# Root mean squares by products with ones on all partitions, and low-key score products over all 128 rows, in a two-layer hybrid decoder

## The chip, the cores and the metric

The kernel runs on one core of a Trainium2 chip. The metric is the device time of one execution of the whole program in microseconds, as a median over runs.

## The reference, cut to what matters

Two decoder layers are applied to a prompt of 1024 tokens and to 8 sample sequences of 4 tokens with 1024 cached ones each. A layer computes a normed input, one combined input projection, four token mixers, four branch projections merged with gates, an output projection and a normed residual. The change touches the root mean square (in the output norm, the next layer's input norm, the per-token layer norm of the convolution branch, and each head of attention) and the scores of the differential attention for the prompt:

```python
def _rms(x, g):
    y = x * lax.rsqrt(jnp.mean(x * x, axis=-1, keepdims=True) + EPS)
    return y * g

def block(args):          # 128 queries, 4 heads, two maps j of width 64
    sc = jnp.einsum('bqhjd,bkhjd->bhjqk', qi, k) * ATTN_SCALE
    sc = jnp.where(kpos <= qpos, sc, -jnp.inf)
    p = jax.nn.softmax(sc, axis=-1)
    return einsum('bhqk,bkhe->bqhe', p[:, :, 0] - lam * p[:, :, 1], v)

o = _rms(attend(q, k, v, lam), g_subln) * (1.0 - lam_init)
```

## The kernel before

Tokens stand in three groups of 352 columns (TB; prompt and samples together make 1056), features on the 128 partitions. TensorE works in fp32 rounded to a shorter format (fp32r) for nearly all of its products, and accuracy comes from splitting: a value is a high part (rounded) and a low part (the rest), and a product is high times high, low times high and high times low. `gemm` (L238) issues such products, `three` lists them, and the tiles `whi_t`, `wlo_t`, `hh_t`, `hl_t` hold the parts of weights and tokens. The weights' ring splits each 128 x 1024 block on ScalarE (L210) and VectorE (L211).

The order of the work on each engine but SyncE is made when the program is built: a scheduler plays the program through on a timeline of its own costs and writes each engine's row of instructions. TensorE then runs its row strictly in order. The source code decides dependences and priorities, and generators (`side`, `step_side`) feed attention and decode between the projections' products. `pace` adds an order between two TensorE products without a wait on data.

Attention of one head is `attn(h)`. `a_part(qb)` makes the scores of 128 queries against n = 128 (qb + 1) keys, in tiles S[0] and S[1] of PSUM for the two maps. The queries and keys of map j lie in `qs[j]` and `ks[j]` over 128 rows: the product takes the high and low parts of the queries against the high keys in one pass. The mask is added by a product of an identity with a mask tile (`identr`, `maskr`). What is missing is the high queries against the low keys. The low keys of both maps share one tile `kl`, map 0 in rows 0 to 63 and map 1 in rows 64 to 127, so this third product has 64 rows for each map, and the two maps' products stand last, beside each other. There are 4 heads of 8 blocks in each of the 2 layers, 64 blocks in all. In six of the eight heads the two maps' low products stand together on TensorE; in the third head of each layer, which runs beside decode, they stand singly.

`rstd_of` gives 1/rms for every column. Before, TensorE multiplies 128 or 88 columns at a time with a vector of ones (L349, in fp32), which puts the sums of squares on partitions; ScalarE takes the square root (L351), VectorE the reciprocal (L352), its high and low part (L355, L356) and two diagonal matrices (L360), and two products of ones with these (L364) spread the result over all partitions. It is called 16 times in attention (512 columns), 6 times each in the layer norm (L1097) and the output norm (L1216), three times for the next layer's input norm (L1223), three times at the start (L1260) and four times in decode (L793, 64 columns). In attention the squares are taken on ScalarE behind each output product (L623).

Of the kernel before, what the change touches and what calls it, by code (L numbers as in the profile page):

```python
# [98 lines left out]
def step_kernel(ctx, tc, xT, wst, wada, kc, vc, ptab, stp, sts, stc, cT, vecs, wpool, lamqk, cst, rope,  # L99
# [221 lines left out]
    def make_A(l, k=0, n=KC):  # L321
        g = cv("g_pre", l, k, n).unsqueeze(2).to_broadcast([P, n, 9])
        ve.scalar_tensor_tensor(out=Am[:, k:k + n], in0=modT[l][:, 8 + k:8 + k + n], scalar=1.0, in1=g, op0=ALU.add, op1=ALU.mult)
# [18 lines left out]
    def rstd_of(x, n, scale, dg, pb=None):  # L342


        w = max(w_ for w_ in (P, TB // 4, 64) if n % w_ == 0)
        m = n // w
        pc = ms(m)[:w]
        for j in range(m):
            te.matmul(out=pc[:, j:j + 1], lhsT=x[:, j * w:(j + 1) * w], rhs=ones[:, 0:1], start=True, stop=True)  # L349
        r = const("rsm", 8, bufs=2)[:w, 0:m]  # L350
        sc.activation(out=r, in_=pc, func=AF.Sqrt, bias=epsc[:w], scale=scale)  # L351
        ve.reciprocal(out=r, in_=r)  # L352
        rs = [r] if len(dg) == 1 else [const(f"rsm{i}", 8)[:w, 0:m] for i in range(2)]
        if len(dg) == 2:
            ve.tensor_copy(out=R(rs[0]), in_=r)  # L355
            ve.tensor_tensor(out=R(rs[1]), in0=r, in1=rs[0], op=ALU.subtract)  # L356
        cast = R if len(dg) == 2 else lambda ap: ap
        for r, d in zip(rs, dg):
            d = d[:w].rearrange("p (j t) -> p j t", t=w)
            ve.tensor_tensor(out=cast(d), in0=ident[:w, :w].unsqueeze(1).to_broadcast([w, m, w]),  # L360
                             in1=r.unsqueeze(2).to_broadcast([w, m, w]), op=ALU.mult)
        pb = ms(n) if pb is None else pb
        for i, d in enumerate(dg):
            te.matmul(out=pb, lhsT=cast(ones[:w]), rhs=cast(d[:w]), start=i == 0, stop=i == len(dg) - 1)  # L364
        return pb
# [57 lines left out]
    def setup_lambda(l, lq):  # L423
# [9 lines left out]
        for o, name, f, w in ((0, "pool_scale", 0.5, 4), (4, "g_cnorm", 0.5, 4), (8, "b_cnorm", 0.5, 4),  # L433
                              (12, "g_subln", 0.5 * (1.0 - lam_init), 1)):
# [4 lines left out]
    def layer(l, pos, hh, hl, begun, psB):  # L439
# [120 lines left out]
        def attn(h):  # L560
            E = [[ep(f"e{2 * i + j}", 1024) for j in range(2)] for i in range(2)]
            wt = [ep(f"e{4 + i}", 4, 256) for i in range(4)]
            od, msq = ep("od", 1056), ep("ms", 1024)
# [4 lines left out]
            def a_part(qb):  # L568
# [5 lines left out]
                chunks = [(c0, min(512, n - c0)) for c0 in range(0, n, 512)]  # L574
                for j in range(2):
                    for c0, w in chunks:
                        c = slice(c0, c0 + max(w, 256))
# [6 lines left out]
                for c0, w in chunks:  # L584
                    c = slice(c0, c0 + max(w, 256))
# [30 lines left out]
            def pv(s):  # L616
# [6 lines left out]
                sc.activation(out=msq[:, s * 256:s * 256 + 256], in_=pb, func=AF.Square)  # L623
# [28 lines left out]
        def decode(p):  # L652
# [428 lines left out]
        def layernorm():  # L1081
            for b in range(3):
# [14 lines left out]
                rs = rstd_of(s2, TB, 1.0 / 512, [lnp("ls1", TB), lnp("ls3", TB)])  # L1097
# [343 lines left out]
```

## Time and profile before

| | |
|---|---|
| median of 3 runs | 3004.43 us (3002.55 to 3007.85) |
| profiled execution, its own time | 3002.23 us |
| its span in the trace | 3000.4 us |
| granted TensorE clock, mean | 0.989 of full speed |
| HBM read, written | 240.73 MB, 36.34 MB |
| instructions in the span | 46185 |

In the views that follow, PE is TensorE's products, PEld its weight loads, DVE VectorE, ACT ScalarE, POOL GpSimd and SP SyncE. A row of a timeline has the start in us, the busy time of the group, the engine, the line, the operation, output and inputs by the program's tile names, for products rows x columns of the weights, the output's shape, and the count of instructions. A group of "lines" ends with busy time in us and the mean duration of one in ns, then the idle time of the engine ahead of them and what ended it. Products on TensorE overlap in a pipeline, so busy times of neighbouring rows overlap as well, and starts are the surer measure. A product in plain fp32 is recorded as two, since it makes two passes.

### The profile page before, as it was taken

The page shows a single profiled execution, that of the slowest core. Times are in us where ns is not written, and L with a number is a line of the kernel's source. Part 1 is how long each engine was busy: PE and PEld are TensorE (multiplying, and loading weights), DVE is VectorE, ACT ScalarE, POOL GpSimd, SP SyncE. Part 2 cuts the span into 40 slices and gives each one's busy share as a digit, 9 for nine tenths or more (in the row PEclk, how much of TensorE's full clock was granted, in tenths as well). Part 3 has the DMA queues.
Part 4 walks back from the last instruction along what each step waited for, and adds up shares of the span by engine and source line. Part 5 has one row for each costly group of instructions (what it writes and reads, how often), then busy time and mean ns, then how long its engine had stood idle before and what let it go on. Part 6 is the DMA issues. An engine that isn't in the chain of part 4 may idle for free.

```text
span 3000.4 us, 46185 instructions
## 1 busy us (share of the span) xinstructions
PE 2913.8 (97%) x18436; PEld 2781.6 (93%) x18436; DVE 1634.2 (54%) x2540; ACT 970.6 (32%) x1904; POOL 495.1 (17%) x642
## 2 busy tenths in 40 slices
PE   6999999999999999999989999999999999999998
PEld 4899889989999999999989998998899999999998
DVE  7756356577972145323487663664889522543233
ACT  4544245313112123212454551542221121322132
POOL 3221011012200111011230120101140001110123
PEclk8999999999999999999999999999999999999999
DMA  6122621362233223222321236115511221221122
GB/s 230 48 65 85 203 78 53 116 196 64 67 109 105 80 86 96 97 75 71 108 98 48 67 118 205 49 45 153 179 38 59 84 76 43 80 90 57 50 69 97
DMA packets 135961, 280.08 MB, mean 93 GB/s; under 512 B 18338, under 2 KB 88994, under 8 KB 134210
## 3 DMA queue, kind: packets, MB, share of 16 engines
q10 hardware_dynamic: 45072, 145.74, 15.9%
q1 hardware_dynamic: 79778, 90.73, 9.7%
q0 software_dynamic: 10896, 40.67, 3.6%
q8 instruction: 145, 2.38, 0.3%
q14 instruction: 70, 0.57, 0.1%
HBM read 240.73 MB, written 36.34 MB: 92 GB/s over the span
## 4 chain that ended last, share of the span: by engine, by line
PE 84%; DVE 7%; DMA 2%; issue 2%; SPq 2%; ACT 2%; POOL 0%; DVEq 0%; ACTq 0%; POOLq 0%
PE mm_t L238 45%; PE m_t L238 28%; PE s_t L238 3%; PE ms_t L238 2%; DVE acc_t L954 2%; SPq L671 1%; PE ms_t L611 1%; PE s_t L776 1%; DVE wlo_t L211 1%; PE s_t L702 1%; DVE acc_t L373 1%; DMA e_t<-in_kc_dram 1%; PE ms_t L349 1%; PE b_t L238 1%; ACT rop_t L497 1%
## 5 line engine op out<-in xcount | busy, mean ns | idle before, releaser
L238 PE MATMUL mm_t<-hh_t,whi_t 128*128 128x352 f32 x2792 | 533.3, 329 | 5.8 <-ACT hh_t L385 2.1
L238 PE MATMUL mm_t<-hh_t,wlo_t 128*128 128x352 f32 x2792 | 528.6, 327 | 0.0
L238 PE MATMUL mm_t<-hl_t,whi_t 128*128 128x352 f32 x2792 | 524.0, 325 | 0.0
L211 DVE TENSOR_TENSOR wlo_t<-wst_t,whi_t 128x1024 fp32r<-128x1024 f32 x203 | 268.5, 1329 | 455.6 <-ACT whi_t L210 455.4
L238 PEld LDWEIGHTS mm_t<-hh_t,whi_t 128*128 128x128 f32 x2792 | 458.7, 190 | 27.6 <-issue 14.6
L238 PEld LDWEIGHTS mm_t<-hh_t,wlo_t 128*128 128x128 f32 x2792 | 460.5, 189 | 9.7 <-issue 8.2
L238 PEld LDWEIGHTS mm_t<-hl_t,whi_t 128*128 128x128 f32 x2792 | 458.7, 189 | 6.7 <-issue 5.6
L954 DVE SCALAR_TENSOR_TENSOR acc_t<-uc_t,vec_t,acc_t 128x1024 f32<-128x1024 f32 x240 | 320.4, 1360 | 1.6
L1164 POOL TENSOR_TENSOR mg_t<-mg_t,th_t 128x352 f32<-128x352 f32 x144 | 144.7, 1008 | 925.8 <-DVE th_t L1163 925.7
L210 ACT ACTIVATE whi_t<-wst_t 128x1024 fp32r<-128x1024 f32 x203 | 213.3, 1056 | 246.7 <-PE mm_t L238 163.6
L238 PE MATMUL m_t<-hh_t,wlo_t 128*128 128x352 f32 x1352 | 249.7, 325 | 0.0
L238 PE MATMUL m_t<-hl_t,whi_t 128*128 128x352 f32 x1352 | 247.6, 324 | 0.0
L238 PE MATMUL m_t<-hh_t,whi_t 128*128 128x352 f32 x1352 | 246.4, 323 | 0.0
L238 PEld LDWEIGHTS m_t<-hh_t,wlo_t 128*128 128x128 f32 x1352 | 223.6, 190 | 0.9
L238 PEld LDWEIGHTS m_t<-hl_t,whi_t 128*128 128x128 f32 x1352 | 222.7, 189 | 0.0
L238 PEld LDWEIGHTS m_t<-hh_t,whi_t 128*128 128x128 f32 x1352 | 222.0, 189 | 0.1
L1072 ACT ACTIVATE th_t<-m_t 128x352 f32<-128x352 f32 x114 | 52.6, 463 | 373.4 <-PE m_t L238 362.5
L1072 ACT ACTIVATE th_t<-mm_t 128x352 f32<-128x352 f32 x78 | 35.9, 463 | 272.0 <-PE mm_t L238 240.9
L590 DVE TENSOR_REDUCE sml_t<-s_t 128x1 f32<-128x256 f32 (+7 forms) x128 | 92.4, 752 | 53.1 <-PE s_t L238 52.7
L593 ACT ACTIVATE e_t<-s_t,sml_t 128x256 f32<-128x256 f32 (+7 forms) x128 | 94.3, 744 | 69.7 <-DVE sml_t L591 39.9
L238 PE MATMUL m_t<-yh_t,whi_t 128*128 128x352 f32 x460 | 94.5, 326 | 0.0
L238 PE MATMUL m_t<-yh_t,wlo_t 128*128 128x352 f32 x460 | 93.1, 324 | 0.0
(349 smaller groups left out, 3854.0 us busy)
## 6 DMA issues: line engine op xcount, KB each, us to landing
wst_t<-in_wst_dram ACTq DMA_DIRECT2D x209, 512.0 KB, 3.6
e_t<-in_kc_dram SPq DMA_DIRECT2D x224, 128.0 KB, 3.0
e_t<-in_vc_dram SPq DMA_DIRECT2D x216, 128.0 KB, 2.6
rld_t<-ysp_t ACTq DMA_DIRECT2D x16, 528.0 KB, 4.5
wa_t<-in_wada_dram SPq DMA_DIRECT2D x16, 512.0 KB, 10.4
wlo_t<-in_wada_dram ACTq DMA_DIRECT2D x16, 512.0 KB, 3.7
whi_t<-in_wada_dram ACTq DMA_DIRECT2D x16, 512.0 KB, 4.3
x_t<-in_xT_dram SPq DMA_DIRECT2D x3, 1408.0 KB, 6.0
```

Of the source, the lines that this page charges most:

```text
L210: sc.activation(out=R(hi), in_=st, func=AF.Copy)
L211: (eng or ve).tensor_tensor(out=R(lo), in0=st, in1=hi, op=ALU.subtract)
L238: last_mm[0] = m = te.matmul(out=out, lhsT=R(lh), rhs=R(rh), start=first and i == 0, stop=last and i == n - 1)
L349: te.matmul(out=pc[:, j:j + 1], lhsT=x[:, j * w:(j + 1) * w], rhs=ones[:, 0:1], start=True, stop=True)
L373: ve.tensor_reduce(out=acc[:, i], in_=o.rearrange("p k n -> p n k"), axis=AX.X, op=ALU.add)
L497: sc.activation(out=sw[32 * (g ^ 1):32 * (g ^ 1) + 32], in_=pb[32 * g:32 * g + 32], func=AF.Copy)
L590: ve.tensor_reduce(out=s[:, j:j + 1], in_=S[j][:, :n], axis=AX.X, op=ALU.max)
L593: sc.activation(out=E[qb % 2][j][:, :n], in_=S[j][:, :n], func=AF.Exp, bias=s[:, 2 + j:3 + j], scale=0.125, accum_out=s[:, 4 + j:5 + j])
L611: te.transpose(out=pb[:, k], in_=e0[:, (k0 + k) * P:(k0 + k + 1) * P], identity=ident)
L954: pace(ve.scalar_tensor_tensor(out=a, in0=v, scalar=w(k), in1=a, op0=ALU.mult, op1=ALU.add))
L1072: sc.activation(out=th[:, b * TB:(b + 1) * TB], in_=pb, func=AF.Tanh, scale=0.5)
L1164: gp.tensor_tensor(out=mg[:, d, cl], in0=mg[:, d, cl], in1=th, op=ALU.add)
```

## The change

Scores: a tile `qz` of 128 rows holds the high queries of map j in that map's rows and zeros in the other map's rows. GpSimd clears it once for each head, and ScalarE copies the queries of the block into it, two copies for each block. The low-key product of map j then runs over all 128 rows of `kl`, and stands directly behind that map's product and mask. It is no longer ordered by `pace` behind both maps. `qz` lies in the tile "ms", which held the squares.

Root mean squares: the squares x are scaled and rounded on ScalarE (high part), VectorE makes the low part, and two products with a full matrix of ones put the sum of each column on all partitions (L356). For the start and decode there is one fp32 product with ones and a scale. ScalarE takes the inverse square root and its square, and VectorE makes one Newton step in place, in PSUM; the factor -0.5 of that step is moved into the following multiplications and constants. In attention the squares are now taken over 512 columns at the end of the head, out of the attention output `od`.

```diff
-    def rstd_of(x, n, scale, dg, pb=None):
-        w = max(w_ for w_ in (P, TB // 4, 64) if n % w_ == 0)
...
-        for j in range(m):
-            te.matmul(out=pc[:, j:j + 1], lhsT=x[:, j * w:(j + 1) * w], rhs=ones[:, 0:1], start=True, stop=True)
...
-        sc.activation(out=r, in_=pc, func=AF.Sqrt, bias=epsc[:w], scale=scale)
-        ve.reciprocal(out=r, in_=r)
...
-        for i, d in enumerate(dg):
-            te.matmul(out=pb, lhsT=cast(ones[:w]), rhs=cast(d[:w]), start=i == 0, stop=i == len(dg) - 1)
+    def rstd_of(x, scale, parts, yt, pb=None):
...
+        if parts:
+            hi, lo = parts
+            sc.activation(out=R(hi), in_=x, func=AF.Copy, scale=scale)
+            ve.scalar_tensor_tensor(out=R(lo), in0=x, scalar=scale, in1=hi, op0=ALU.mult, op1=ALU.subtract)
+            for i in range(2):
+                te.matmul(out=pb, lhsT=R(ones), rhs=R(parts[i]), start=i == 0, stop=i == 1)
+        else:
+            te.matmul(out=pb, lhsT=ones, rhs=x, start=True, stop=True)
+            ve.tensor_scalar(out=pb, in0=pb, scalar1=scale, scalar2=None, op0=ALU.mult)
+        sc.activation(out=y, in_=pb, func=AF.Abs_reciprocal_sqrt, bias=epsc)
+        sc.activation(out=t, in_=y, func=AF.Square)
+        ve.scalar_tensor_tensor(out=pb, in0=pb, scalar=EPS, in1=t, op0=ALU.add, op1=ALU.mult)
+        ve.scalar_tensor_tensor(out=pb, in0=pb, scalar=-3.0, in1=y, op0=ALU.add, op1=ALU.mult)
...
+            qz = ep("ms", 1024)[:, 0:512].rearrange("p (i j q) -> p i j q", i=2, j=2)
+            gp.memset(qz, 0.0)
...
+                for j in range(2):
+                    r = slice(64 * j, 64 * j + 64)
+                    sc.activation(out=R(qz[r, qb % 2, j]), in_=qs[j][r, q1], func=AF.Copy)
                 for j in range(2):
...
                         gemm(S[j][:, c], [(qs[j][:, q1], ks[j][:, c])], last=False)
-                    gemm(S[j][:, q1], [(identr, maskr)], first=False, last=False)
+                        if c is chunks[-1]:
+                            gemm(S[j][:, q1], [(identr, maskr)], first=False, last=False)
+                        gemm(S[j][:, c], [(qz[:, qb % 2, j], kl[:, c])], first=False)
                     if j == 0:
                         yield
-                hi = last_mm[0]
-                for c0, w in chunks:
...
-                    for j in range(2):
-                        r = slice(64 * j, 64 * j + 64)
-                        gemm(S[j][:, c], [(qs[j][r, q1], kl[r, c])], first=False, on=hi)
...
-                sc.activation(out=msq[:, s * 256:s * 256 + 256], in_=pb, func=AF.Square)
...
+                msq = ep(f"e{4 + i}", 1024)[:, 0:512]
+                sc.activation(out=msq, in_=o[:, c], func=AF.Square)
+                rs = rstd_of(msq, 1.0 / P, two(dg), two(yt))
```

Since a scheduler sets the rows, three places show what moved. First TensorE in the third head of the first layer, beside decode's products (`s_t<-e_t` are decode's, `mm_t` are the projection's, `k_t`, `maskr_t` and `kl_t` the score's, `x8` counts equal products in a row). Before:

```order
L238 MATMUL mm_t<-hl_t,whi_t 128x352 x7
L238 MATMUL s_t<-k_t,q_t 128x256
L238 MATMUL s_t<-maskr_t,identr_t 128x128
L238 MATMUL s_t<-kl_t,q_t 128x256
L238 MATMUL mm_t<-hl_t,whi_t 128x352
L238 MATMUL mm_t<-hh_t,whi_t 128x352 x6
L776 MATMUL s_t<-e_t 32x256 x8
L238 MATMUL mm_t<-hh_t,whi_t 128x352 x2
L238 MATMUL mm_t<-hh_t,wlo_t 128x352 x8
```

Now, in the same head:

```order
L238 MATMUL mm_t<-hh_t,wlo_t 128x352 x3
L238 MATMUL s_t<-k_t,q_t 128x256
L238 MATMUL s_t<-maskr_t,identr_t 128x128
L238 MATMUL s_t<-kl_t,ms_t 128x256
L238 MATMUL s_t<-k_t,q_t 128x256
L238 MATMUL s_t<-maskr_t,identr_t 128x128
L238 MATMUL s_t<-kl_t,ms_t 128x256
L238 MATMUL mm_t<-hh_t,wlo_t 128x352 x5
L238 MATMUL mm_t<-hl_t,whi_t 128x352
L611 MATMUL ms_t<-cs_t,e_t 128x128
```

A map used to stand by itself between decode's products; now both maps of a block stand together, with nothing of decode's between, and the low-key product reads the tile of zeros (`ms_t`).

Second, ScalarE in the first head, where the exponentials (L593) follow the scores. Before:

```order
L210 ACTIVATE whi_t<-wst_t 128x1024
L506 ACTIVATE k_t<-rop_t 64x352 x2
L593 ACTIVATE e_t,sml_t<-s_t,sml_t 128x128 x2
L541 ACTIVATE vcm_t<-mm_t 128x352
L210 ACTIVATE whi_t<-wst_t 128x1024
L506 ACTIVATE q_t<-tbb_t 64x352 x2
```

Now, with the query copies (L580):

```order
L210 ACTIVATE whi_t<-wst_t 128x1024
L580 ACTIVATE ms_t<-q_t 64x128 x2
L541 ACTIVATE vcm_t<-mm_t 128x352
L210 ACTIVATE whi_t<-wst_t 128x1024
L593 ACTIVATE e_t,sml_t<-s_t,sml_t 128x128 x2
L506 ACTIVATE k_t<-rop_t 64x320 x2
L513 ACTIVATE knew_t<-rop_t 128x32
L497 ACTIVATE tbb_t<-mm_t 32x352 x4
L210 ACTIVATE whi_t<-wst_t 128x1024
L580 ACTIVATE ms_t<-q_t 64x128 x2
L593 ACTIVATE e_t,sml_t<-s_t,sml_t 128x256
```

The copies of a block stand behind a weights' copy (L210), and in the second block ahead of the exponentials.

Third, TensorE at the end of the first layer, the output norm of the last group of tokens (`ada_t`). Before:

```order
L349 MATMUL ms_t<-ones_t,ssq_t 88x1 x4
L238 MATMUL mm_t<-hh_t,whi_t 128x352 x8
L238 MATMUL mm_t<-hh_t,wlo_t 128x352 x8
L238 MATMUL mm_t<-hl_t,whi_t 128x352 x8
L238 MATMUL mm_t<-hh_t,whi_t 128x352 x8
L238 MATMUL mm_t<-hh_t,wlo_t 128x352 x8
L364 MATMUL ada_t<-acc_t,ones_t 128x352
L238 MATMUL mm_t<-hl_t,whi_t 128x352 x2
L364 MATMUL ada_t<-acc_t,ones_t 128x352
```

Now:

```order
L356 MATMUL ada_t<-parts_t,ones_t 128x352
L238 MATMUL mm_t<-hh_t,whi_t 128x352 x8
L238 MATMUL mm_t<-hh_t,wlo_t 128x352 x8
L238 MATMUL mm_t<-hl_t,whi_t 128x352 x8
L238 MATMUL mm_t<-hh_t,whi_t 128x352 x5
L356 MATMUL ada_t<-parts_t,ones_t 128x352
L238 MATMUL mm_t<-hh_t,whi_t 128x352 x3
```

The four column products are gone, and the two halves of the remaining product, which stood two products apart at the end, now stand 29 products apart.

More of the change, by code (lines that the diff above doesn't have):

```diff
@@ L322, in make_A @@
         g = cv("g_pre", l, k, n).unsqueeze(2).to_broadcast([P, n, 9])
-        ve.scalar_tensor_tensor(out=Am[:, k:k + n], in0=modT[l][:, 8 + k:8 + k + n], scalar=1.0, in1=g, op0=ALU.add, op1=ALU.mult)
+        a = Am[:, k:k + n]
+        ve.scalar_tensor_tensor(out=a, in0=modT[l][:, 8 + k:8 + k + n], scalar=1.0, in1=g, op0=ALU.add, op1=ALU.mult)
+        ve.tensor_scalar(out=a, in0=a, scalar1=-0.5, scalar2=None, op0=ALU.mult)
     def make_G(l):
@@ L340, in two @@
         return [t[:, 0], t[:, 1]]
[L342 to L364 removed]
+    def rstd_of(x, scale, parts, yt, pb=None):
+        n = x.shape[-1]
+        y, t = yt
+        pb = ms(n) if pb is None else pb
+        if parts:
[11 more added lines that the diff above has]
+        ve.scalar_tensor_tensor(out=pb, in0=pb, scalar=-3.0, in1=y, op0=ALU.add, op1=ALU.mult)
         return pb
@@ L644, in attn @@
                 c = slice(i * 512, i * 512 + 512)
-                dg = ep(f"e{i}", 1024)
-                rs = rstd_of(msq[:, c], 512, 1.0 / P, two(dg.rearrange("p (i n) -> p i n", i=2)))
+                dg, yt = [ep(f"e{i + x}", 1024).rearrange("p (i n) -> p i n", i=2) for x in (0, 2)]
+                msq = ep(f"e{4 + i}", 1024)[:, 0:512]
+                sc.activation(out=msq, in_=o[:, c], func=AF.Square)
+                rs = rstd_of(msq, 1.0 / P, two(dg), two(yt))
                 ve.tensor_tensor(out=o[:, c], in0=o[:, c], in1=rs, op=ALU.mult)
@@ L789, in decode @@
             sc.activation(out=fin, in_=pb, func=AF.Copy)
-            sqd, rsd = wn[:, 0:64], wn[:, 64:128]
+            sqd, yd = wn[:, 0:64], wn[:, 64:128]
             sc.activation(out=sqd, in_=pb, func=AF.Square)
             yield
-            ve.tensor_tensor(out=fin, in0=fin, in1=rstd_of(sqd, 64, 1.0 / P, [rsd]), op=ALU.mult)
+            ve.tensor_tensor(out=fin, in0=fin, in1=rstd_of(sqd, 1.0 / P, None, (yd, qf)), op=ALU.mult)
             ve.scalar_tensor_tensor(out=fin, in0=fin, scalar=hv[:, l, 12:13],
@@ L1096, in layernorm @@
                 yield from skip(6)
-                rs = rstd_of(s2, TB, 1.0 / 512, [lnp("ls1", TB), lnp("ls3", TB)])
-                ve.tensor_tensor(out=x, in0=x, in1=rs.unsqueeze(1).to_broadcast([P, 4, TB]), op=ALU.mult)
+                rs = rstd_of(s2, 1.0 / 512, [lnp(f"lr{i}", TB) for i in range(2)], [t[:, i] for i in range(2)])
+                ve.scalar_tensor_tensor(out=x, in0=rs.unsqueeze(1).to_broadcast([P, 4, TB]), scalar=-0.5, in1=x,
+                                        op0=ALU.mult, op1=ALU.mult)
                 for c in range(4):
@@ L1215, in layer @@
                 ve.tensor_tensor(out=scols(ob[:, :, n:]), in0=scols(ob[:, :, n:]), in1=samp(GG), op=ALU.mult)
-            rs = rstd_of(ssq, TB, 1.0 / D, two(op("acc", 2, TB)), psM("ada", 512)[:, 0:TB])
+            rs = rstd_of(ssq, 1.0 / D, two(op("parts", 2, TB)), two(op("yt", 2, TB)), psM("ada", 512)[:, 0:TB])
             for d in range(0, KC, 2):
                 o_, x_ = ob[:, d:d + 2], xb[:, d:d + 2]
-                ve.tensor_tensor(out=o_, in0=o_, in1=rs.unsqueeze(1).to_broadcast([P, 2, TB]), op=ALU.mult)
+                ve.scalar_tensor_tensor(out=o_, in0=rs.unsqueeze(1).to_broadcast([P, 2, TB]), scalar=-0.5, in1=o_,
+                                        op0=ALU.mult, op1=ALU.mult)
                 (gp if d % 4 else ve).tensor_tensor(out=x_, in0=x_, in1=o_, op=ALU.add)
@@ L1222, in layer @@
                 gp.dma_start(out=xmid[b], in_=xb)
-                rs = rstd_of(sumsq(xb, ob, op("acc", 2, TB)), TB, 1.0 / D, two(op("acc", 2, TB)))
+                rs = rstd_of(sumsq(xb, ob, op("acc", 2, TB)), 1.0 / D, two(op("parts", 2, TB)), two(op("yt", 2, TB)))
                 for t, x in zip(nh, "hl"):
```

12 lines of the change are left out of this document (5 added, 7 removed).

## The prediction

> **What bounds the kernel now.** I read the page first, then the busy time by stages, then TensorE's timeline at each kind of work that the change touches, then the groups by line for the prices on the other engines, and last the end of the program. The page, engines' busy time:
>
> ```profile
> PE 2913.8 (97%) x18436; PEld 2781.6 (93%) x18436; DVE 1634.2 (54%) x2540; ACT 970.6 (32%) x1904; POOL 495.1 (17%) x642
> ```
>
> and its chain of work that ended last:
>
> ```profile
> PE 84%; DVE 7%; DMA 2%; issue 2%; SPq 2%; ACT 2%; POOL 0%; DVEq 0%; ACTq 0%; POOLq 0%
> ```
>
> PE works for 97% of the span and makes 84% of the chain. So a microsecond taken off PE's row of work comes off the end, as long as the other engines keep up; and steps added to DVE or ACT cost nothing unless PE stands waiting for them. The busy time by stages (columns: busy time of PE, PEld, DVE, ACT, POOL, granted clock, DMA share, GB/s) for the end of the first layer and the stretch behind it:
>
> ```profile
> 1440.00:1500.00 60.00, 60.00 (x385) 59.98 (x384) 28.67 (x41) 25.75 (x47) 16.72 (x15) 1.00 0.27 93
> 1500.00:1600.00 100.00, 88.30 (x533) 84.33 (x533) 82.00 (x153) 55.84 (x125) 33.05 (x45) 0.93 0.27 93
> ```
>
> Inside a layer PE has no gap at all. At the transition between layers it stands idle for 11.7 us of 100 and DVE is busy for 82: there, longer chains on DVE and ACT do show.
>
> **Low-key products: what goes.** TensorE's timeline in the second head, first where the two maps of a block stand together over 256 keys, then over 640 keys (512 and 256 columns). Columns: start, busy time, operation, tiles, rows times columns of the weights, output, count. Busy times of pipelined products overlap, so I take start to start:
>
> ```profile
> 199.62 1.46 PE L238 MATMUL mm_t<-hl_t,whi_t 128*128 128x352 f32 x8
> 200.92 0.28 PE L238 MATMUL s_t<-k_t,q_t 128*128 128x256 f32 x1
> 201.03 0.23 PE L238 MATMUL s_t<-maskr_t,identr_t 128*128 128x128 f32 x1
> 201.09 0.33 PE L238 MATMUL s_t<-k_t,q_t 128*128 128x256 f32 x1
> 201.26 0.22 PE L238 MATMUL s_t<-maskr_t,identr_t 128*128 128x128 f32 x1
> 201.41 0.38 PE L238 MATMUL s_t<-kl_t,q_t 64*128 64x256 f32 x2
> 201.73 1.56 PE L238 MATMUL mm_t<-hh_t,whi_t 128*128 128x352 f32 x8
> 203.13 1.46 PE L238 MATMUL mm_t<-hh_t,wlo_t 128*128 128x352 f32 x8
> ...
> 227.74 0.51 PE L238 MATMUL s_t<-k_t,q_t 128*128 128x512 f32 x2
> 228.09 0.22 PE L238 MATMUL s_t<-maskr_t,identr_t 128*128 128x128 f32 x1
> 228.24 0.61 PE L238 MATMUL s_t<-kl_t,q_t 64*128 64x512 f32 x4
> 228.78 1.08 PE L238 MATMUL mm_t<-hh_t,wlo_t 128*128 128x352 f32 x5
> 229.70 0.60 PE L611 MATMUL ms_t<-cs_t,e_t 128*128 128x128 f32 x4
> ```
>
> A plain product of 352 columns takes 1.30/8 = 0.162 us, one of 256 columns 0.11 to 0.12, 512 and 256 together 0.35, so one of 512 takes 0.23; for 384 I take 0.18, between them. A mask product ahead of a full-row product takes 0.06 (201.03 to 201.09); ahead of 64-row products it takes 0.15 (201.26 to 201.41; 228.09 to 228.24). So entering costs 0.09. The pair of 64-row products takes 0.32 (201.41 to 201.73), where one full-row product of that width takes 0.12: 0.20 on top. Behind them eight products take 1.40 instead of 1.30, five take 0.92 instead of 0.81: leaving costs 0.10 to 0.11. Together about 0.40 us for a group. The wider pairs bear it out: 0.54 against 0.35, again 0.19 on top.
>
> In the third head of each layer the maps stand singly, with one 64-row product in a group:
>
> ```profile
> 403.94 0.22 PE L238 MATMUL s_t<-maskr_t,identr_t 128*128 128x128 f32 x1
> 404.09 0.38 PE L238 MATMUL s_t<-kl_t,q_t 64*128 64x256 f32 x1
> 404.40 0.58 PE L238 MATMUL mm_t<-hh_t,whi_t 128*128 128x352 f32 x2
> 404.82 0.97 PE L238 MATMUL mm_t<-hh_t,wlo_t 128*128 128x352 f32 x5
> ```
>
> Again 0.15 ahead, 0.31 within, and 0.42 for two products instead of 0.32. A single costs as much as a pair, so the pair runs side by side in the array, and that is what the change gives up. There are 6 heads with 8 joined blocks and 2 heads with 16 single maps, 80 groups: 80 x 0.40 = 32.0 us go. In the 6 joined heads each pair becomes two products in a row. The blocks' widths, 256 twice, 384, 512, 512+256 twice, 512+384 and 512+512, make 0.12 + 0.12 + 0.18 + 0.23 + 0.35 + 0.35 + 0.41 + 0.46 = 2.22 us a head, 13.3 in all. In the third heads nothing is added. **Net: -18.7 us.**
>
> This is also where a rule stands for and against. By the Trainium skill's page "TensorEngine Tiling (Array Packing)", section Tiling Modes, a change of tiling mode drains TensorE, while tiles of one mode work independently. The rows show both: 0.09 ahead and 0.10 behind, and a pair for the price of a single. By the second half alone (a pair is free parallelism to be kept) the sum of the low-key part would be +13.3 instead of -18.7.
>
> **Root mean squares on PE.** In attention, at the end of the fourth head (four columns in two passes each make eight records):
>
> ```profile
> 561.29 0.95 PE L349 MATMUL ms_t<-ones_t,ms_t 128*128 128x1 f32 x8
> 562.10 1.54 PE L238 MATMUL mm_t<-hl_t,whi_t 128*128 128x352 f32 x8
> ...
> 567.02 0.39 PE L364 MATMUL ms_t<-e_t,ones_t 128*128 128x512 f32 x1
> 567.26 0.50 PE L349 MATMUL ms_t<-ones_t,ms_t 128*128 128x1 f32 x4
> ```
>
> and for the tokens at the layer transition:
>
> ```profile
> 1533.30 0.71 PE L349 MATMUL ms_t<-ones_t,ssq_t 128*88 128x1 f32 x8
> 1534.02 1.56 PE L238 MATMUL mm_t<-hh_t,whi_t 128*128 128x352 f32 x8
> 1535.41 1.46 PE L238 MATMUL mm_t<-hh_t,wlo_t 128*128 128x352 f32 x8
> ...
> 1540.58 0.33 PE L364 MATMUL ada_t<-acc_t,ones_t 88*128 88x352 f32 x1
> 1540.75 0.49 PE L238 MATMUL mm_t<-hl_t,whi_t 128*128 128x352 f32 x2
> ```
>
> A call in attention spends 0.81 on the columns and 2 x 0.24 on spreading the result; the new one spends two products of 512 columns, 0.46. Saved: 0.83, times 16 calls (8 heads, two halves) 13.3 us. A token call loses its 0.72; its two spreading products (0.17 each) are replaced by two of the same width (0.162). With 6 layer norms and 6 output norms that is 12 x 0.72 = 8.6. Leaving fp32 costs the products behind it 1.39 - 1.30 = 0.09; in the two orders PE passes from fp32 back to rounded products 177 times before and 143 after: 34 x 0.09 = 3.1. The 3 norms of the next layer's input may give up to 2 more, which I leave at zero, as they stand where PE waits anyway; the start and decode calls trade like for like. **Net: -25.0 us.**
>
> **Other engines.** The nearest rows for the new steps are the same forms elsewhere, a rounding copy and the rest of it for 352 columns, and the weights' copy that may stand ahead of them:
>
> ```profile
> L1133 ACT ACTIVATE hh_t<-mg_t 128x352 fp32r<-128x352 f32 x48 | 20.6, 488 | 21.6 <-POOL mg_t L1164 14.9 <-PE mm_t L238 3.4 <-PE m_t L238 3.4
> L1134 DVE SCALAR_TENSOR_TENSOR hl_t<-mg_t,hh_t 128x352 fp32r<-128x352 f32 x48 | 24.0, 552 | 9.9 <-ACT hh_t L1133 9.9
> L210 ACT ACTIVATE whi_t<-wst_t 128x1024 fp32r<-128x1024 f32 x203 | 213.3, 1056 | 246.7 <-PE mm_t L238 163.6 <-PE m_t L238 82.1 <-DMA od_t<-in_vc_dram 0.5
> ```
>
> A call has copy, rest, two products, inverse root, square and two DVE steps in a row: 0.49 + 0.55 + 0.33 + 2 x 0.49 + 2 x 0.52 = 3.4 us. The old chain, at the very end:
>
> ```profile
> 2985.74 0.52 DVE L1211 TENSOR_TENSOR ssq_t<-ssq_t,sq_t 128x352 f32<-128x352 f32 x1
> ```
>
> to the first use of the result,
>
> ```profile
> 2989.62 3.28 DVE L1219 TENSOR_TENSOR ob_t<-ob_t,ada_t 128x704 f32<-128x704 f32 x4 [0.75 <-PE ada_t L364]
> ```
>
> takes 3.4 us from the end of the sum. With waits between the steps I count **+0.5** here (0 to +1). At the transition the order puts the second half product of the last output norm 29 products behind the first, 4.7 us, and 99 products behind the previous block's against 88 before: 11 x 0.162 = 1.8, and about 2 us of ACT and DVE behind it (2 x 0.49 + 2 x 0.52), less what the idle 11.7 us take up: **+3** (0 to +4). The start, where one inverse root follows a product: **+0.5** (0 to +2). The query copies, 128 on ACT at less than 0.49 each, and POOL's zeros for each head, lie beside PE: ACT is 32% busy, POOL 17%. The squares, 16 instructions of 512 columns in place of 32 of 256, now stand at the head's end; nothing but the head's store and its tiles waits for them. The copies can be late for a low product now and then, and the third heads are packed tighter: **+2** (0 to +10). K pages of decode load into the e tiles that attention frees; once PE waited for them:
>
> ```profile
> 608.92 2.14 PE L702 MATMUL s_t<-e_t 128*32 128x512 f32 x16 [2.34 <-DMA e_t<-in_kc_dram]
> ```
>
> Now the tiles come free with less PE work ahead, but more of them serve the root: 0, with -5 to +5 as ends, about twice that wait.
>
> **Sum.** -18.7 - 25.0 + 0.5 + 3 + 0.5 + 2 = -37.7 us. The profiled execution took 3002.2, 2.2 under the median of 3004.4; against the median the forecast is 3004.4 - 37.7, about **2967 us**.
>
> **Rivals.** (a) *The third heads give their part back.* In them the order sets a block's copy and low products close together, 15 to 29 products (2.4 to 4.7 us) between blocks, where single maps used to be spread among decode's work, and the tile of zeros is also decode's, so that the head starts late. Then their 32 x 0.40 = 12.8 are lost and some 3 us of waits come: 2967 + 16 = 2983. For it: the crowding in the order. Against it: copies of 0.49 fit into 2.4 us. Chance 0.13.
> (b) *The 0.40 doesn't belong to the 64 rows* but to any product onto a bank that the mask has just written, and stays. Then low-key costs +13.3, and 25.0 - 13.3 - 6 leaves -5.7: 2999. Against it: a k product right behind a mask starts after 0.06. Chance 0.07. The second half of the rule of the Trainium skill's page "TensorEngine Tiling (Array Packing)", section Tiling Modes, taken alone, gives the same 2999.
> (c) *Slower: the low product waits for the query copy.* PE is in order; all products of the layer queue behind it. If ACT takes the copy behind one weights' copy, 1.06 us, in each of 64 blocks, 68 us come and the kernel lands at 2967 + 68 = 3035. It decides from 37.7/64 = 0.6 us of wait for each block. Against it: ACT's order has the copies of a block ahead of the exponentials of the one before, and ACT is idle for two thirds. Chance 0.07.
> (d) *Nothing comes through*: the pace is set by weights or by DVE, and PE's savings turn into gaps. For it: DVE's 82% at the transition. Against it: no gap in 60 us ahead of it. About 3004, chance 0.05.
>
> **How the numbers follow.** The forecast keeps 0.68. A measurement here can tell about 0.2%, 6 us, from no change. Faster: the forecast and (a), 0.81; same: (b) and (d), 0.12; slower: (c), 0.07. Of the unknown costs the good ends (transition, end, start and waits at zero, -6; K loads -5; the norms left at zero -2; 0.45 instead of 0.40 a group, -4) give 2950. The bad ends without K loads' come to +11 (transition +1, end +0.5, start +1.5, waits +8): 2978, and 2983 of (a) with half of the rest, +9, 2992. So 2950 to 2992; (b), (c) and (d), 0.19, lie outside.
>
> **What would show it.** In the profile after: no 64-row low products left, a mask ahead of a low product at 0.06 to 0.1 and products behind at 0.162; L349's groups gone; PE's busy time down by some 40 us and its share still near 97%. Wrong would be: PE waiting for the ms tile from ACT in front of low products (c), waits in the third heads (a), low products that still take 0.3 us (b), or a larger idle time at the transition than 11.7 + 3.

## The result, and the profile after

The changed kernel takes 2984.25 us (median of 4 runs, 2983.43 to 2984.78), the kernel before 3003.49 beside it; the ratio is 0.9933, with a 95% interval of 0.9916 to 0.9951. That is 19 us less, where 37.7 were forecast. A second set on another chip (e11 below) gave 0.9951 (0.9937 to 0.9965), so the gain is 14 to 20 us. In the profiled executions the span falls from 3000.4 to 2981.7 us, by 18.7.

The page of the changed kernel, engines' busy time, and its chain:

```profile
PE 2878.0 (97%) x18156; PEld 2767.8 (93%) x18156; DVE 1634.6 (55%) x2488; ACT 1062.3 (36%) x2089; POOL 504.4 (17%) x650
...
PE 81%; DVE 8%; ACT 5%; SPq 2%; issue 2%; DMA 2%; POOL 0%; ACTq 0%; DVEq 0%; POOLq 0%
```

TensorE's busy time fell from 2913.8 to 2878.0, by 35.8 us; 43.7 had been summed. What TensorE stands idle, the span less its busy time, rose from 86.6 to 103.7, by 17.1; 6 had been allowed for. The two misses, 7.9 and 11.1, are the 19 us that didn't come. ACT's share of the chain rose from 2% to 5%.

Where the idle time is, by windows of before (columns as in the prediction: busy time of PE, PEld, DVE, ACT, POOL, granted clock, DMA share, GB/s):

```profile
0.00:62.00 62.00, 40.99 (x194) 24.05 (x195) 39.74 (x60) 25.90 (x38) 14.84 (x19) 0.83 0.65 256
445.00:600.00 155.00, 153.64 (x996) 144.72 (x995) 94.08 (x194) 67.60 (x142) 18.84 (x40) 1.00 0.27 83
...
1930.00:2070.00 140.00, 136.71 (x889) 130.75 (x891) 86.29 (x183) 66.35 (x140) 17.56 (x38) 1.00 0.22 69
2560.00:2680.00 120.00, 119.63 (x747) 118.71 (x746) 70.51 (x73) 39.94 (x56) 20.40 (x22) 1.00 0.28 93
```

and of the changed kernel:

```profile
0.00:62.00 62.00, 36.41 (x167) 20.03 (x168) 40.75 (x61) 26.46 (x39) 13.92 (x19) 0.89 0.65 256
445.00:600.00 155.00, 147.92 (x941) 139.28 (x941) 90.82 (x182) 77.68 (x156) 17.20 (x37) 0.98 0.31 98
1500.00:1600.00 100.00, 84.70 (x504) 81.97 (x504) 80.67 (x147) 61.14 (x141) 28.09 (x43) 0.91 0.26 92
1930.00:2070.00 140.00, 133.72 (x852) 125.51 (x851) 77.73 (x159) 69.63 (x140) 11.08 (x28) 0.98 0.33 101
2560.00:2680.00 120.00, 116.14 (x715) 115.19 (x714) 55.97 (x64) 40.64 (x59) 25.84 (x23) 1.00 0.26 84
```

TensorE's idle time grew by 4.6 us in the start, 5.7 where the third head of the first layer ends and the fourth begins, 3.6 at the transition, 3.0 at the second layer's fourth head, and 3.5 where its layer norms stand: 20.4 together, while other places lost some. A window is fixed in time, so work that drops out of it counts as idle time there: at the start the first product of the projections begins only 1.2 us later (`b_t`, 37.63 instead of 36.46), and the rest of the 4.6 us are products that are gone. In both fourth heads the granted clock goes from 1.00 to 0.98 as well. The Trainium skill, on the page "TensorE: Matmul & The Clock Gate", section HAM oscillation, says that a wait of TensorE which is long enough is followed by a start at a lower clock; the trace agrees in its sense, since in both these windows more idle time and the lower clock come together (the longest single wait there is 3.2 us).

What ScalarE does in the first of these fourth heads, on its timeline (changed kernel):

```profile
474.42 1.28 ACT L361 ACT_TABLE_LOAD   x1
475.71 0.69 ACT L361 ACTIVATE e_t<-ms_t,epsc_t 128x512 f32<-128x512 f32 x1
476.30 0.30 ACT L580 ACTIVATE ms_t<-q_t 64x128 fp32r<-64x128 f32 x1
476.61 1.28 ACT L593 ACT_TABLE_LOAD   x1
477.91 0.37 ACT L593 ACTIVATE e_t<-s_t,sml_t 128x128 f32<-128x128 f32 x1
...
479.24 1.28 ACT L361 ACT_TABLE_LOAD   x1
480.53 0.69 ACT L361 ACTIVATE e_t<-ms_t,epsc_t 128x512 f32<-128x512 f32 x1
...
482.86 1.28 ACT L593 ACT_TABLE_LOAD   x1
484.15 0.37 ACT L593 ACTIVATE e_t<-s_t,sml_t 128x128 f32<-128x128 f32 x1
```

and TensorE at the same time, the rows with idle time ahead of them:

```profile
478.42 0.38 PE L238 MATMUL s_t<-k_t,q_t 128*128 128x256 f32 x1 [0.91 <-ACT e_t L593]
...
484.66 0.38 PE L238 MATMUL s_t<-k_t,q_t 128*128 128x256 f32 x1 [3.21 <-ACT e_t L593]
...
487.42 0.69 PE L238 MATMUL s_t<-k_t,q_t 128*128 128x384 f32 x1 [1.92 <-ACT e_t L593]
```

The inverse roots of the third head's two halves (L361) and the first two exponentials of the fourth (L593) alternate, and each needs another table: four loads of 1.28 us within ten microseconds. The next block's scores can't overwrite a score tile before its exponential has read it, and TensorE, in order, stands in front of them for 6.0 us.

The low-key products as they run now:

```profile
472.21 0.28 PE L238 MATMUL s_t<-k_t,q_t 128*128 128x256 f32 x1
472.33 0.22 PE L238 MATMUL s_t<-maskr_t,identr_t 128*128 128x128 f32 x1
472.39 0.34 PE L238 MATMUL s_t<-kl_t,ms_t 128*128 128x256 f32 x1
472.56 1.29 PE L238 MATMUL mm_t<-hh_t,wlo_t 128*128 128x352 f32 x7
473.68 0.39 PE L356 MATMUL ms_t<-e_t,ones_t 128*128 128x512 f32 x1
```

As forecast the mask's slot is 0.06 and the products behind run at 1.12/7 = 0.160. But the low-key product's own slot is 0.17, not the 0.12 of a product of that width (the k product ahead of the mask takes 0.12). The mask's short slot is made up by its successor.

At the end of the program, the last sum and the first use of the norm:

```profile
2966.25 0.52 DVE L1213 TENSOR_TENSOR ssq_t<-ssq_t,sq_t 128x352 f32<-128x352 f32 x1
...
2970.86 3.28 DVE L1221 SCALAR_TENSOR_TENSOR ob_t<-ada_t,ob_t 128x704 f32<-128x704 f32 x4
```

4.1 us instead of 3.4: the +0.5 of the prediction was 0.7.

### The profile page after: what moved, and what is told of

Same layout as the page of the kernel before. It is cut to its first block, busy times and chain, and to the rows that moved or that the text cites. A ratio compares the mean times of both kernels' runs of the same rounds, so it can differ in the third digit from the quotient of the medians.

```text
span 2981.7 us, 45818 instructions
## 1 busy us (share of the span) xinstructions
PE 2878.0 (97%) x18156; PEld 2767.8 (93%) x18156; DVE 1634.6 (55%) x2488; ACT 1062.3 (36%) x2089; POOL 504.4 (17%) x650
## 4 chain that ended last, share of the span: by engine, by line
PE 81%; DVE 8%; ACT 5%; SPq 2%; issue 2%; DMA 2%; POOL 0%; ACTq 0%; DVEq 0%; POOLq 0%
PE mm_t L238 43%; PE m_t L238 28%; PE s_t L238 3%; DVE acc_t L955 2%; PE ms_t L238 2%; SPq L672 2%; PE ms_t L611 1%; ACT rop_t L497 1%; PE s_t L777 1%; DVE wlo_t L211 1%; SPq L409 1%; PE s_t L703 1%; DVE acc_t L373 1%; DMA e_t<-in_kc_dram 1%; PE ada_t L300 1%
## 5 line engine op out<-in xcount | busy, mean ns | idle before, releaser
L210 ACT ACTIVATE whi_t<-wst_t 128x1024 fp32r<-128x1024 f32 x203 | 213.4, 1056 | 276.5 <-PE mm_t L238 195.1
L593 ACT ACTIVATE e_t<-s_t,sml_t 128x256 f32<-128x256 f32 (+7 forms) x128 | 94.1, 739 | 48.3 <-DVE sml_t L591 46.9
L238 PE MATMUL m_t<-yl_t,whi_t 128*128 128x352 f32 x460 | 93.2, 324 | 0.0
```

The costliest lines, as they stand in the source:

```text
L210: sc.activation(out=R(hi), in_=st, func=AF.Copy)
L238: last_mm[0] = m = te.matmul(out=out, lhsT=R(lh), rhs=R(rh), start=first and i == 0, stop=last and i == n - 1)
L593: sc.activation(out=E[qb % 2][j][:, :n], in_=S[j][:, :n], func=AF.Exp, bias=s[:, 2 + j:3 + j], scale=0.125, accum_out=s[:, 4 + j:5 + j])
```

## The experiments

The first theory was that the missing time lies mostly in waits, made by ScalarE's alternating tables at the fourth heads; the rivals were that the products were saved less than summed, that the roots' longer chains cost time wherever they stand, and that the query copies hold products up. Runs e1 to e4, e5 to e8 and e9 to e12 shared one set of runs of the kernel before each (medians 3000.45, 3000.09 and 3002.55), so that ratios compare across them better than times. Busy and idle are TensorE's, in the profiled execution.

Busy time has a part that belongs to the clock. Each trace lists stretches in which the granted clock was one half; in them a product of 352 columns takes 0.30 us from start to start instead of 0.163. Half of TensorE's busy time in these stretches is taken here as lost to the clock, which is an estimate: 19.9 us before, 22.1 in the changed kernel, 22.7 in e1, 22.2 in e2, 23.9 in e3, 25.1 in e4, 19.3 in e5, 34.8 in e8 and 19.8 in e12. "Without the clock" below means busy time less this. Most of the edits also made the scheduler write another row for TensorE: against the kernel that it was made from, e3's differs at 1165 of 18156 places, e7's at 606, e8's at 1361 and e9's at 1809, e5's at none, and e12's from e1's at 10 of 18436.

| run | median us | ratio to before (95%) | span | busy | idle | table loads |
|---|---|---|---|---|---|---|
| before | 3003.49 | | 3000.4 | 2913.8 | 86.6 | 46 |
| changed | 2984.25 | 0.9933 (0.9916-0.9951) | 2981.7 | 2878.0 | 103.7 | 50 |
| e1 low-key part | 2996.76 | 0.9986 (0.9977-0.9995) | 2995.1 | 2901.8 | 93.3 | 50 |
| e2 norm part | 2987.69 | 0.9955 (0.9941-0.9968) | 2983.7 | 2890.1 | 93.6 | 46 |
| e3 roots first | 2977.22 | 0.9920 (0.9906-0.9933) | 2975.6 | 2878.0 | 97.6 | 42 |
| e4 64 rows, single | 3042.59 | 1.0138 (1.0123-1.0154) | 3040.5 | 2947.3 | 93.2 | 46 |
| e5 no tables | 2962.99 | 0.9875 (0.9860-0.9890) | 2957.7 | 2871.8 | 85.9 | 1 |
| e6 no mask | 2963.94 | 0.9875 (0.9861-0.9890) | 2962.1 | 2862.7 | 99.4 | 42 |
| e7 no copies | 2969.48 | 0.9892 (0.9877-0.9906) | 2973.6 | 2878.8 | 94.8 | 42 |
| e8 more tables | 3020.51 | 1.0065 (1.0052-1.0077) | 3019.0 | 2889.0 | 130.0 | 77 |
| e9 steps in SBUF | 2994.31 | 0.9974 (0.9963-0.9985) | 2992.5 | 2882.2 | 110.3 | 42 |
| e10 the same, not e3 | 2996.52 | 0.9979 (0.9970-0.9988) | 2994.7 | 2887.1 | 107.6 | 50 |
| e11 changed again | 2988.70 | 0.9951 (0.9937-0.9965) | 2986.9 | 2881.0 | 105.9 | 50 |
| e12 e1, roots first | 2992.23 | 0.9968 (0.9956-0.9980) | 2988.4 | 2899.1 | 89.3 | 46 |

**e1, the low-key part alone.** The new `a_part` in the kernel before, with its old `rstd_of`; the squares are taken at the head's end, since the zeros need their tile.

> Only the low-key products over 128 rows (with the squares taken at the head's end, as there the tile is needed for the zeros); the root mean squares as before. First theory (the missing microseconds of the change are waits in the fourth heads, where ScalarE alternates between the root and the exponential and loads a table each time; the products themselves were saved nearly as summed): work on TensorE falls by 13 to 19 us, but here too one exponential stands between the two roots of the third head's end, so 10 to 20 us come back: 2995 to 3010 us. Second theory (no such waits; the low-key part simply saved next to nothing or all of its 18.7): 2985 if the sum of the prediction holds, 3003 if the group's 0.40 us stayed, in both cases without idle time of TensorE at the start of the fourth heads.

4 us came (ratio 0.9986). Busy time fell by 12.0 (14.8 without the clock), idle time rose by 6.7. The first theory's range holds the time, the second's two values don't. But the first theory's reason fails: ScalarE alternates at the third head's end here too (four loads from 471.58 to 484.28), and TensorE waits for the exponentials there only 0.6 us, and 0.9 in the second layer:

```profile
486.54 0.69 PE L238 MATMUL s_t<-k_t,q_t 128*128 128x384 f32 x1 [0.62 <-ACT e_t L592]
```

**e2, the norm part alone.** The changed kernel with the old `a_part`.

> Only the root mean squares changed; low-key products on 64 rows, both maps last, as before. In this order both roots of a head's end stand together on ScalarE. First theory (waits from alternating tables): the prediction's own sum for this part, -25.0 + 4 = -21, or some more, 2975 to 2983 us, as nothing alternates. Second theory (the root mean squares' longer chains on ScalarE and VectorE eat the gain everywhere): a gain of 10 us at most, 2993 us or more.

13.5 us came, between the two. Busy time fell by 23.7 (26.0 without the clock), close to the 25.0 of the prediction, and idle time rose by 7.0. Both roots stand together, with one load, and TensorE still waits 3.2 us for the first exponential of the fourth head, in both layers:

```profile
485.04 0.39 PE L238 MATMUL s_t<-k_t,q_t 128*128 128x256 f32 x1 [3.19 <-ACT e_t L594]
```

So alternation alone (e1) makes next to none of these waits, and the norm part without it (e2) about half of what the changed kernel has there; with both in one kernel there are 6.0. Together e1 and e2 give busy -35.7, the whole change -35.8: the two parts add up on TensorE's busy side.

**e3, both roots ahead of the next exponential.**

```diff
-        sc.activation(out=y, in_=pb, func=AF.Abs_reciprocal_sqrt, bias=epsc)
+        root[0] = sc.activation(out=y, in_=pb, func=AF.Abs_reciprocal_sqrt, bias=epsc)
...
+                    pace(ex, root[1]) if qb + j == 0 and root[1] else None
...
-                rs = rstd_of(msq, 1.0 / P, two(dg), two(yt))
+                rs, root[1] = rstd_of(msq, 1.0 / P, two(dg), two(yt)), root[0]
```

`ex` is the exponential's instruction.

> The changed kernel with one more order: the first exponential of the next head stands behind both roots of the head before on ScalarE; nothing else. First theory: the waits at the start of the fourth heads (about 6 us each) and the slower clock behind them (about 4 us each) go in both layers, 20 us less than the changed kernel: 2960 to 2970 us, and 42 table loads instead of 50. Rival (TensorE waits there for the query copies or for the keys, and the alternation only lies beside it): 2980 to 2987 us.

2977.2 us: less than the changed kernel (by the ratios 4 to 9 us; against e11 the intervals part, against the first set they overlap), with the same busy time to the tenth and 6.1 us less idle. So the alternation costs about 6 us in this kernel, together with what the new row of TensorE changes, and not the 20 that I gave it. In the fourth head TensorE now waits like this:

```profile
481.77 0.39 PE L238 MATMUL s_t<-k_t,q_t 128*128 128x256 f32 x1 [1.19 <-ACT e_t L593]
...
482.64 0.39 PE L238 MATMUL s_t<-k_t,q_t 128*128 128x256 f32 x1 [0.25 <-ACT e_t L593]
...
485.58 1.89 PE L526 MATMUL ms_t<-cs_t,vcm_t 128*128 128x128 f32 x6 [2.10 <-DVE od_t L648]
```

Of 6.0 us 3.5 are left, and 2.1 of them are a new wait, for the bank of PSUM in which the two steps on VectorE work.

**e4, single products on 64 rows.**

```diff
-                        gemm(S[j][:, c], [(qz[:, qb % 2, j], kl[:, c])], first=False)
+                        gemm(S[j][:, c], [(qs[j][r, q1], kl[r, c])], first=False)
```

> The changed kernel, but each low-key product uses the 64 rows of its own map in the queries, standing where the full-row product stands (the copies are still made and not read). 192 products each form a group of their own. If going to 64 rows and back costs about 0.34 us for a group (0.20 within, 0.10 behind, 0.04 ahead), 65 us come to the changed kernel; both roots stand together in this order, so some 20 us of waits go: about 3029 us, 3049 if the waits stay. Rival (the extra time belongs to any product behind the mask or to the tile it adds onto, not to the rows): within 5 us of the changed kernel's 2984, or 2964 without the waits.

Busy time rose by 69.3 over the changed kernel, 69.3/192 = 0.36 us a group (66.4 and 0.35 without the clock); the time by 56 to 62 by the ratios, as idle time fell by 10.5. The time lies between the two that were expected, since only half of the 20 us of waits went. TensorE's rows show the price directly:

```profile
211.39 0.22 PE L238 MATMUL s_t<-maskr_t,identr_t 128*128 128x128 f32 x1
211.54 0.38 PE L238 MATMUL s_t<-kl_t,q_t 64*128 64x256 f32 x1
211.85 0.38 PE L238 MATMUL s_t<-k_t,q_t 128*128 128x256 f32 x1
212.07 0.22 PE L238 MATMUL s_t<-maskr_t,identr_t 128*128 128x128 f32 x1
```

The slots of mask, low-key product and the k product behind are 0.15, 0.31 and 0.22, where full rows have 0.06, 0.17 and 0.12: 0.33 us more. The price of a group on 64 rows is confirmed, and belongs to the rows: the same product behind the same mask, onto the same bank, costs it when the rows are exchanged.

**e5, no table loads.** e3 with `AF.Tanh` in place of `AF.Abs_reciprocal_sqrt` in `rstd_of`.

> The kernel with both roots ahead of the next head's exponential (e3), with one function of ScalarE exchanged: the inverse root becomes a hyperbolic tangent, which lies in the exponential's table, so that 1 table load is left of 42. This leaves the normalisation out (what comes out is not 1/rms). TensorE's row of instructions stays the same. First theory (what still costs at the heads' ends and at the layer transition is ScalarE's table loads): the 3.6 us of waits at each fourth head and the clock behind them shrink, 6 to 12 us less than e3's 2977, about 2968. Rival (the longer chains themselves, copy, rest, products, square and two steps on VectorE, hold TensorE up): within 3 us of e3.

14 us less than e3, somewhat over the first theory's 6 to 12, with TensorE's row of instructions unchanged. Idle time falls by 11.7 and busy time by 6.2, of which 4.6 are the clock's. But the loads aren't all of it. By the lists of TensorE's waits those for the exponentials go (3.0 us in e3), those in the layer norms go (3.6, for `ls_t`), and those for `rop_t` fall from 6.5 to 2.3. At the start and at the transition little changes (e5):

```profile
0.00:62.00 62.00, 35.48 (x167) 19.91 (x168) 40.73 (x61) 25.16 (x37) 13.90 (x19) 0.89 0.65 256
1500.00:1600.00 100.00, 85.02 (x510) 81.89 (x510) 78.28 (x157) 61.60 (x147) 24.11 (x39) 0.91 0.18 63
```

TensorE is idle for 26.5 and 15.0 us there, as in the changed kernel (25.6 and 15.3) and not as before (21.0 and 11.7), and the wait for the bank at the fourth heads stays too (3.8 of 4.2 in both layers). So the rival is right at these places: the new steps hold TensorE up there without any load. That the idle time comes to what it was before, 85.9 and 86.6, is a coincidence of what went and what stayed, since e5 also lacks the 45 loads that the kernel before had beyond its first.

**e6, no mask.** e3 without the two lines of the mask product.

> e3 without the 128 mask products (the causal mask of the diagonal block is left out). If a mask product costs what its own slot of 0.06 us shows, 128 x 0.06 = 7.7 us go: 2969.5. If it costs 0.115, as a product of that many weights does, and hands 0.055 on to the product behind it, 14.7 us go: 2962.5, and the low-key product behind a k product takes 0.117 for 256 columns instead of 0.17.

13.3 us less, busy time 15.3 less: 15.3/128 = 0.12 us a mask, as the second of the two values had it. Its rows show the low-key product behind a k product, and then the next:

```profile
470.59 0.28 PE L238 MATMUL s_t<-k_t,q_t 128*128 128x256 f32 x1
470.71 0.28 PE L238 MATMUL s_t<-kl_t,ms_t 128*128 128x256 f32 x1
470.83 0.48 PE L238 MATMUL mm_t<-hl_t,whi_t 128*128 128x352 f32 x2
```

0.12 instead of 0.17.

**e7, no copies.** e3 without the three lines of the query copies.

> e3 without the 128 query copies on ScalarE: the low-key products read zeros, so the queries' product with the low keys is left out of the scores, while every product still runs. If the copies lie beside TensorE's work, as the prediction counted them: within 3 us of e3's 2977. If low products wait for them, or their place in ScalarE's row holds the exponentials up: 6 us or more less.

The size isn't settled. All four runs (2966.8 to 2975.4) lie below all five of e3 (2976.1 to 2979.7), and the median 7.7 us below e3's; in the profiled ones, 2975.4 and 2977.3, the difference is 2.0, with the same busy time within 0.8. So the copies, or the row of TensorE that comes with them, cost something rather than nothing, about 8 us by the medians and 2 by the profiled executions.

**e8, more tables.**

```diff
-        root[0] = sc.activation(out=y, in_=pb, func=AF.Abs_reciprocal_sqrt, bias=epsc)
+        sc.activation(out=t, in_=pb, func=AF.Ln, bias=epsc)
+        root[0] = sc.activation(out=y, in_=t, func=AF.Exp, scale=-0.5)
```

> e3 with the inverse root made of a logarithm and an exponential, which the build places in two tables: 77 table loads instead of 42, and one more operation in every chain. 35 x 1.28 = 45 us and 34 x 0.5 = 17 us come to ScalarE, which has idle time for them. First theory (tables cost where TensorE waits for ScalarE: four heads' ends, the transition, the layer norms): 10 to 20 us more than e3, about 2992. Rival (tables lie beside the work): 2977 to 2980.

43 us more, over twice the forecast: ScalarE's busy time rose by 65 us (1050.3 to 1114.9), TensorE's idle time by 32.4 and its busy time by 11.0, all of which is the clock's (10.9 by the estimate). ScalarE is 37% busy there, and still two thirds of what was added to it reached the end.

**e9 and e10, the two steps in SBUF.**

```diff
-        ve.scalar_tensor_tensor(out=pb, in0=pb, scalar=EPS, in1=t, op0=ALU.add, op1=ALU.mult)
-        ve.scalar_tensor_tensor(out=pb, in0=pb, scalar=-3.0, in1=y, op0=ALU.add, op1=ALU.mult)
-        return pb
+        ve.scalar_tensor_tensor(out=t, in0=pb, scalar=EPS, in1=t, op0=ALU.add, op1=ALU.mult)
+        ve.scalar_tensor_tensor(out=t, in0=t, scalar=-3.0, in1=y, op0=ALU.add, op1=ALU.mult)
+        return t
```

e9 has e3's order, e10 the changed kernel's.

> e3 with the two steps on VectorE written to the small tile t instead of back into the product's bank of PSUM, so that the bank is free after the first of them. First theory (what is left of the waits at the fourth heads is the bank: the value transposes wait 2.1 us there for the multiplication that reads it last, once in each layer): these waits go, and the step at the layer transition is no longer: 4 to 8 us less than e3, about 2971. Rival (TensorE waits there for the exponentials or the values all the same): within 2 us of e3.

> The changed kernel with the two steps written to the small tile, and without the order of e3: the roots and the exponentials still alternate, 50 table loads. First theory (both causes add up): 2 to 5 us less than the changed kernel, as the exponentials still hold TensorE up: about 2980. Rival (the bank was the whole cause and the alternation only lay beside it): as fast as e9.

Both theories of e9 and e10 fall: both are slower than the kernels they were made from, by about 16 and 8 to 14 us by the ratios. e10 is as fast as e9 within the intervals, as the rival had it, but not for its reason: TensorE waits 9.5 us for the exponentials in e10 and 2.9 in e9, and other waits make up for it. The wait for the bank is gone, but others stand in its place (e9, TensorE in the fourth head and at the transition):

```profile
485.64 0.55 PE L526 MATMUL ms_t<-cs_t,vcm_t 128*128 128x128 f32 x3 [1.41 <-DVE vl_t L530]
...
488.30 0.47 PE L611 MATMUL ms_t<-cs_t,e_t 128*128 128x128 f32 x1 [2.00 <-DVE sml_t L591]
...
1542.64 0.35 PE L238 MATMUL s_t<-k_t,q_t 128*128 128x256 f32 x1 [2.79 <-DVE q_t L509]
```

All three wait for VectorE, whose busy time rose from 1635.0 to 1651.9; GpSimd's rose from 505.6 to 521.0. The second of the two steps, with both inputs in SBUF, and the multiplication that reads the result in the output norm show where (e3, then e9; times in ns are shortest, median and longest):

```profile
L364 DVE SCALAR_TENSOR_TENSOR ms_t<-ms_t,e_t x16: 685/696/700, 171.5 to 2029.5; 128x512 f32<-128x512 f32 x16
L1221 DVE SCALAR_TENSOR_TENSOR ob_t<-ada_t,ob_t x24: 878/879/891, 1456.2 to 2967.2; 128x704 f32<-128x704 f32 x24
```

```profile
L364 DVE SCALAR_TENSOR_TENSOR e_t<-e_t x16: 683/693/1444, 168.4 to 2041.0; 128x512 f32<-128x512 f32 x16
L1221 DVE SCALAR_TENSOR_TENSOR ob_t<-yt_t,ob_t x24: 877/893/2401, 1459.6 to 2982.8; 128x704 f32<-128x704 f32 x24
```

A step out of SBUF alone isn't slower: the median is the same. Four of the 16 steps take 0.99 to 1.44 us, all of them while GpSimd works; in e3 three of the 16, with an input and the output in PSUM, also run beside GpSimd and take 0.69. At L1221, which reads the factor out of SBUF instead of PSUM, the sum of the 24 goes from 21.2 to 33.3 us, which is most of what VectorE gained, and the four at the program's end take 4.77 us instead of 3.28. Whether these longer steps alone moved the waits above, or the new row of TensorE too, isn't shown.

**e11, the changed kernel again,** and **e12, e1 with e3's order.**

> The changed kernel once more, on the chip of these runs: 2981 to 2985 us if this chip runs it as the first one did, and 4 to 8 us over e3.

2988.7 us, 14 below before instead of 19, and 9 to 12 us over e3 (by the ratios and by the medians): both expectations are missed. TensorE's row and its waits for the exponentials are the same as in the first set (12.0 us, 11.8 there). So what separates the changed kernel from e3 is known to a few microseconds only.

> e1 (the low-key products alone, root mean squares as before) with both roots of a head's end ahead of the next head's exponential: 46 table loads instead of 50. First theory (the low-key products save 12 to 14 us of TensorE's work, not the 18.7 of the prediction, since a mask product hands part of its time on): 12 us less than before, about 2988. If the prediction's price was right: 2982. If even here only e1's 4 us come: the alternation wasn't what ate the rest.

2992.2 us by the ratio 0.9968 (-9.6, from -13.2 to -6.0), and -12.0 by the spans. Busy time falls by 14.7 (14.5 without the clock), idle time rises by 2.7. That is the first theory's value within the interval; the 18.7 lie outside. e1 and e12 differ by 4 loads and, with nearly the same row on TensorE, by 4.0 us of idle time and 2.7 of busy time, the latter the clock's; they ran on two chips, and their intervals still overlap. This is the cleanest trial of the order on ScalarE, and it gives less than the 6.1 of e3.

## Why the prediction was right and where it was wrong

The sign and the mechanism on TensorE held; the size came out at half, for three terms. That 2984 lies in the range is partly luck: the forecast's own bad ends went to 2978, and only rival (a), which didn't happen, carried the range on to 2992.

- **Low-key products, -18.7 summed, -12.0 to -14.7 measured** (e1 and e12, busy time; -14.8 and -14.5 without the clock). The failed step is "entering costs 0.09". It compared the mask's slot ahead of 64-row products, 0.15, with its slot ahead of full ones, 0.06, as if 0.06 were a mask's price. It costs 0.115 to 0.12 (e6), and ahead of a full product half of it shows in the successor's slot. So, behind a mask, entering adds about 0.15 - 0.115 = 0.035, a group costs 0.34 instead of 0.40, and 80 x 0.34 - 13.3 = 13.9. Of the 80 groups before, 78 stand behind a mask. Where a k product of 512 columns stands directly ahead, as in 64 of e4's groups, its slot goes from 0.23 to 0.32, so there 0.09 is right. The rest of the step, 0.20 within, 0.10 behind, and a pair for the price of a single, stands: e4 found 0.36, or 0.35 without the clock.
- **Norms on TensorE, -25.0 summed, -23.7 measured** (e2; -26.0 without the clock). The prices held nearly, for the prediction had the start as "like for like", and about 3 us of the saving stand there, where column products went as well. They brought nothing: they stood ahead of a wait, which grew from 4.3 to 8.3 us (`b_t` for `hh_t`).
- **Waits, +6 summed, +17.1 measured.** The transition (+3) was 3.6, the end (+0.5) was 0.7, and the start (+0.5) 1.2 by the first product of the projections (by the windows, 4.6 of idle time); e5 shows that those at the transition and at the start don't come from table loads. What failed is the +2 for copies and crowding, with "ACT is 32% busy" as its cover: the fourth heads gave 8.7 us and the second layer's layer norms, for which the sum has no term, 3.5. The prediction counted the new root as an operation of 0.49 us like the copies. In the trace it is 0.69 over attention's 512 columns, with a table load of 1.28 ahead of it and another behind it, and the order let the next head's exponentials in between. The trace of before had 23 such loads ahead of L351; the sum has no term for them. At the fourth heads e3 takes part of it back by the order, e2 shows that the norm part makes 3.2 us of wait in each without any alternation, and without loads 1.8 to 1.9 us are left in each, the wait for the bank (e5). The layer norms' waits go with the loads.
- **K pages, 0, with -5 to +5**: by the list of TensorE's waits those for `in_kc_dram` fell from 10.1 us to 5.3, so the good end came; it is part of the 3.3 us that places outside the five windows lost.
- **Rivals.** (a) didn't happen: the list of TensorE's waits has none for the copies. (b) is refuted by e4 and by the rows after. (c), a wait of 0.6 us for the copy in each block, didn't happen; e7 leaves 2 to 8 us for all 128 copies and the row that comes with them. (d) was right in a part that I hadn't meant: gaps took back some of the saving, but made by the new steps on ScalarE and VectorE, not by weights.

What stays open: e5 takes all loads but one away, also those that the kernel before had (46), so its 14 us aren't all the change's doing; how they split wasn't tried. Nor was the new order on ScalarE tried with TensorE's row held fixed, but for e1 and e12, so e3's 6 us aren't the order's alone. And e7's spread.

Of the versions that compute the same, e3 is the fastest, with 2977.2 us (0.9920 of before). The Trainium skill's page "ScalarE: Activation LUTs", section Rules for kernel authors, says to group work by table set and to do all of one set before switching. e3 does that in one place, and the trace agrees with its sense; it gives about 2.7 us for a switch, where 1.31 us lie here between the end of the copy (476.60) and the start of the exponential (477.91), 1.283 of them the load.

## What to carry to other kernels

Price a short product by what a row of several takes, not by its own slot: a slot can be short because the next one pays. When work moves into a chain through ScalarE, write down which function stands before and behind it in ScalarE's row and count table loads there, since an engine that is a third busy can still be the one that is waited for; but try the order before believing it, since the loads alone made hardly any wait in e1. A saving on the bounding engine counts only where that engine isn't already waiting.

## What the hardware showed that I had not expected

- A product of 128 columns takes a slot of 0.06 us and hands about 0.055 on to its successor: 0.17 for 256 columns behind it, 0.12 behind another product of 256.
- 65 us of added work on ScalarE, most of it table loads, made a program longer by 43 us (e8) in which ScalarE has idle time for two thirds of the span, and TensorE's mean granted clock fell from 0.986 to 0.980.
- A step on VectorE over 128x512 took 0.69 us with both inputs in SBUF, as long as with an input and the output in PSUM; but four of 16 took 0.99 to 1.44 us while GpSimd worked, and at L1221 the longest went from 0.89 to 2.40 us (e9 and e3).
